# Q times K transposed for 96 heads: twelve-head blocks loaded one by one, or eight-head blocks loaded in pairs

## The chip, the cores and the metric

The kernel runs on one core of one Trainium2 chip. The metric is the device time of one execution in microseconds (us). Before the change the median of three runs is 1062.25 us (1062.21 to 1062.76). One more execution was profiled: it took 1061.68 us, and its span from the first to the last instruction is 1059.7 us, so 2.0 us lie around the span.

## The reference

```python
batch, n_heads, seq, head_dim = 8, 12, 1024, 64
q, k: float32 [8, 12, 1024, 64]

def reference(q, k):
    return np.einsum('bhid,bhjd->bhij', q, k).astype(np.float32)
```

For each of the 96 heads this is a 1024 x 1024 matrix of float32, 4 MB (4096 KB as the profile counts transfers). The inputs are 50.3 MB in all, the output is 402.7 MB.

## The kernel before

**Blocks of heads.** The 96 heads are worked in order. They are grouped in blocks (`sizes`, L33): 2, 2, 4, 8, 8 and then six blocks of 12. A block is what is loaded, cast and transposed together. The heads of one block are computed while the next block is being prepared.

**Loads.** The first three blocks are loaded into a tile `early` that borrows one of the three output buffers, the first two head by head (`load_head`), the third whole. From the fourth block on, `load` (L70 to L80) takes one of the two buffers of `in_pool` and moves Q, or K, of the whole block with one DMA. Each of the 128 partitions gets `N*S/128` consecutive rows of 64 floats, so one contiguous piece of 16 KB in a block of eight and of 24 KB in a block of twelve. Block 3 is loaded at the start, Q from SP's queue and K from ACT's. All later loads stand in a list `stream`; `next_load` takes the next one and issues it from ACT's queue. Two are taken (Q and K of one block) in one place of each block, given by `LOADS` (L353): head 1 of block 2, head 4 of blocks 3 and 4, head 6 of the later ones, always behind the second of that head's four copies on ACT. A load into a buffer waits until GpSimd has cast everything that was in it, and this wait stands in ACT's own instruction order: the copies behind it wait too.

**Casts.** GpSimd (POOL) turns a loaded block into float16, in chunks (`cast_quads`, L117 to L137). `cut` (L68) says into how many row groups a block is divided, so that a chunk fits a tile of `CHUNK` = 1536 float16 a partition; with two parts for each of Q and K that is eight chunks for a block of 8 or of 12. A chunk is four casts of 32 partitions. Chunks go to tiles of `half_pool`, of which there are five. `to_half` puts the casts into GpSimd's program as far as two blocks ahead.

**Transposes.** VectorE (DVE) transposes each chunk in 32 x 32 squares (`transpose_quads`, L143 to L149) into `qT` or `kT`, of which there are two sets (`tr_pool`), so that block i+1 is prepared while block i is read. VectorE's program holds nothing else but a few early copies. The first transpose of a block waits until TensorE has finished with the block two before it.

**Scores and stores.** For each head TensorE makes 16 matmuls of 128 x 512 (L175), two 1024-column rows of PSUM tile at a time; ACT copies 128 x 2048 from PSUM to `o_sb` four times (L185); SP then stores the head's 4 MB with one DMA of 128 pieces of 32 KB (L189). There are three `o_sb` buffers, so the copies of a head wait for the store of the head three before it. The seventh head from the end (`SPLIT`) is stored in parts from several queues (`split_scores`), one of them from a tile of `in_pool`.

Of the kernel before, what the change touches and what calls it, by code (L numbers as in the profile page):

```python
# [9 lines left out]
F32 = mybir.dt.float32  # L10
P = 128

@with_exitstack
def kernel(
# [6 lines left out]
    nc = tc.nc  # L21

    B, H, S, D = q.shape
    NT = S // P
    BH = B * H
# [3 lines left out]
    qf = q.rearrange("b h s d -> (b h s) d")  # L29
    kf = k.rearrange("b h s d -> (b h s) d")  # L30
    of = out.rearrange("b h i j -> (b h) i j")

    sizes = [2, 2, 4, 8, 8] + [12] * ((BH - 24) // 12)  # L33
    assert sum(sizes) == BH
    PE_BLOCKS = 2
    NMAX = max(sizes)
    CHUNK = 48 * 32
    SPLIT = BH - 7
    KEEP = 6

# [3 lines left out]
    spare = consts.tile([P, P], F16)  # L44

    in_pool = ctx.enter_context(tc.tile_pool(name="in_pool", bufs=2))
    half_pool = ctx.enter_context(tc.tile_pool(name="half_pool", bufs=5))
    tr_pool = ctx.enter_context(tc.tile_pool(name="tr_pool", bufs=2))
    out_pool = ctx.enter_context(tc.tile_pool(name="out_pool", bufs=3))

    pin = tc.keep_in_program_order

    def half_tile():
        half_sb = half_pool.tile([P, CHUNK], F16, tag="half")
        return half_sb

    class Block:
# [3 lines left out]
        def __init__(self, first, N, by_pe):  # L61
            self.first, self.N, self.by_pe = first, N, by_pe
            self.R = N * S // P
            self.elems = self.R * D
            self.raw = [None] * 2
            self.rows = [None] * 2
            self.halves = {}
            self.cut = max(1, self.R * 32 // CHUNK + (self.R * 32 % CHUNK > 0))  # L68

        def load(self, x, eng):  # L70
            if self.raw[x] is None:
                x_sb = in_pool.tile([P, self.elems], F32, tag="x")
                self.raw[x] = x_sb
            start = self.first * S
            src = (qf, kf)[x][start : start + self.N * S]
            pin(
                eng.dma_start(  # L77
                    out=self.raw[x], in_=src.rearrange("(p r) d -> p (r d)", p=P)
                )
            )  # L80

# [113 lines left out]
    def split_scores(b, n, ps_pool):  # L195
        half, g = divmod(n, b.N // 2)
        cs = slice(half * D, (half + 1) * D)
        qT = b.qT[cs, g * S : (g + 1) * S]
        kT = b.kT[cs, g * S : (g + 1) * S]
        dst = of[b.first + n]  # L200
        o_sb = out_pool.tile([P, NT, S], F32, tag="out")
        more_sb = in_pool.tile([P, NMAX * S // P * D], F32, tag="x")

        sorted_sb = half_tile()
        kept = KEEP * P
        groups = qT[:, kept:].rearrange("c (e s r t) -> c s t e r", s=2, r=4, t=4)
        columns = sorted_sb[cs, : 4 * P].rearrange("c (t m) -> c t m", t=4)
        for m in range(4):
            pin(
                nc.vector.tensor_copy(  # L210
                    out=columns[:, :, 32 * m : 32 * m + 32].rearrange(
                        "c t (e r) -> c t e r", r=4
                    ),
                    in_=groups[:, 1 - m // 2],
                )
            )
        for_five = slice(0, 64)
        pin(
            nc.gpsimd.dma_start(
                out=spare[:5, for_five].rearrange("p (a x) -> p a x", a=2)[:, :, :16],  # L220
                in_=ident[:5, for_five].rearrange("p (a x) -> p a x", a=2)[:, :, :16],
            )
        )

        def rows(to, count, weights, copy):
            ps = ps_pool.tile([P, 2 * S], F32, tag="po")
            for m, w in enumerate(weights):
                for j in range(2):
                    at = m * S + j * 512
                    pin(  # L230
                        nc.tensor.matmul(  # L231
                            ps[:count, at : at + 512], w, kT[:, j * 512 : j * 512 + 512]
                        )
                    )
            pin(copy(out=to, in_=ps[:count, : len(weights) * S]))  # L235

        flat = o_sb.rearrange("p t j -> p (t j)")
        first = qT[:, :kept].rearrange("c (p t) -> c t p", t=KEEP)
        for u in range(0, KEEP, 2):
            rows(  # L240
                flat[:, u * S : (u + 2) * S],
                P,
                [first[:, u], first[:, u + 1]],
                nc.scalar.copy,
            )
        pin(
            nc.sync.dma_start(
                out=dst[:kept].rearrange("(p t) j -> p (t j)", t=KEEP),
                in_=flat[:, : KEEP * S],
            )  # L250
        )
        for u in range(2):
            rows(
                more_sb[:, 3 * u * S : (3 * u + 2) * S],
                P,
                [columns[:, 2 * u], columns[:, 2 * u + 1]],
                nc.scalar.copy,
            )
        pairs = more_sb.rearrange("p (u t j) -> p u (t j)", u=2, j=S)[:, :, : 2 * S]
        blocks_of = dst[kept:].rearrange("(e s r t) j -> s e r (t j)", s=2, r=8, t=2)  # L260

        def part(eng, side, first, last):
            base = 64 * (1 - side)
            pin(
                eng.dma_start(  # L265
                    out=blocks_of[side, first:last],
                    in_=pairs[base + 4 * first : base + 4 * last],
                )
            )

        part(nc.gpsimd, 1, 5, 8)
        part(nc.gpsimd, 0, 0, 8)
        part(nc.sync, 1, 0, 4)
        left = kept + 9 * 16
        rows(flat[:16, KEEP * S : KEEP * S + S], 16, [qT[:, left : left + 16]], nc.scalar.copy)
        pin(nc.sync.dma_start(out=dst[left : left + 16], in_=flat[:16, KEEP * S : KEEP * S + S]))

    blocks, first = [], 0
# [7 lines left out]
    for b in blocks[:3]:  # L286
# [7 lines left out]
        else:  # L294
            for x in range(2):
                b.load(x, (nc.sync, nc.scalar)[x])
    stream = [(b, x) for b in blocks[3:] for x in range(2)]

    def next_load(eng):
        if stream:  # L300
            b, x = stream.pop(0)
            b.load(x, eng)

    for x in range(2):
        next_load((nc.sync, nc.scalar)[x])
    make_identity(nc, ident)

    casts = [
# [3 lines left out]
    def to_half(last):  # L312
        while casts:
            i, c = casts[0]
            if i > last or (blocks[i], c[0]) in stream:
                return
            blocks[i].cast_quads(*c)
            casts.pop(0)

    for b in blocks[:PE_BLOCKS]:  # L320
        for x in range(2):
            b.cast_rows(x)
    to_half(2)

    def block(i, heads, ps_pool, w):
        b = blocks[i]
        nxt = blocks[i + 1] if i + 1 < len(blocks) else None
        for n in heads:
            side = {}
            if nxt and nxt.by_pe:  # L330
                if n == 1:
                    side = {
                        u: [
                            lambda x=u // 2: nxt.transpose_rows(
                                x, ps_pool, nc.vector.tensor_copy
                            )
                        ]
                        for u in (1, 3)
                    }
            elif nxt:  # L340
                parts = nxt.chunks()
                some = [s for m, s in enumerate(parts) if m * b.N // len(parts) == n]
                side = {0: [lambda s=s: nxt.transpose_quads(*s) for s in some]}

            if n == LOADS.get(i, 6):
                side[1] = side.get(1, []) + [lambda: next_load(nc.scalar)] * 2
            if b.first + n == SPLIT:
                split_scores(b, n, ps_pool)
            else:
                b.scores(n, side, ps_pool, w)  # L350
            to_half(i + 2 + (n == b.N - 1))

    LOADS = {0: None, 1: None, 2: 1, 3: 4, 4: 4}  # L353

    blocks[0].alloc()
    blocks[1].alloc()
    with tc.tile_pool(name="first_pool", bufs=4, space=bass.MemoryType.PSUM) as pool:
        for x in range(2):
            blocks[0].transpose_rows(x, pool, (nc.vector.tensor_copy, nc.scalar.copy)[x])
        block(0, [0], pool, 1)  # L360
    po_pool = ctx.enter_context(
        tc.tile_pool(name="po_pool", bufs=2, space=bass.MemoryType.PSUM)
    )
    block(0, [1], po_pool, 2)
    for i in range(1, len(blocks)):
        if i + 1 < len(blocks):
            blocks[i + 1].alloc()
        block(i, range(blocks[i].N), po_pool, 2)
# [30 lines left out]
```

## Time and profile before

| what | value |
| --- | --- |
| median of three runs | 1062.25 us |
| profiled execution | 1061.68 us |
| its span | 1059.7 us |
| bytes read from and written to memory | 50.33 MB and 402.65 MB |
| mean rate over the span | 427 GB/s |
| store of a head: issues, size, median time from issue to landing | 95, 4096 KB, 21.8 us |
| load of a twelve-head Q: issues, size, median time to landing | 6, 3072 KB, 22.8 us |
| load of a twelve-head K: issues, size, median time to landing | 6, 3072 KB, 39.9 us |
| matmul L175, mean of 1520 | 617 ns |
| copy L185, 128 x 2048, mean of 376 | 1869 ns |
| cast L131, 32 x 1536, mean of 192 | 1460 ns |
| transpose L149, 128 x 1536, mean of 24 each for Q and K | 8065 and 8121 ns |

The engines' busy times overlap. A share of the span says how much an engine worked, not that it set the pace. MB are millions of bytes; the KB of a transfer are 1024 bytes. In the list of DMA queues q1 is the queue that SP issues to and q10 the one of ACT; "share of 16 engines" is the time of their packets over sixteen times the span.

### The profile page before, as it was taken

How to read it: one execution, taken by the hardware profiler on the slowest of the kernel's cores; microseconds unless marked ns; L12 is line 12 of the kernel's file. 1: busy time of each engine (PE TensorE's matmuls, PEld its weight loads, DVE VectorE, ACT ScalarE, POOL GpSimd, SP SyncE). 2: the span in 40 equal slices, each digit the busy share in tenths (PEclk: the TensorE clock that was granted, in tenths of full speed). 3: DMA queues.
4: the chain of work that ended last, by engine and by line, in shares of the span. 5: the costliest groups of instructions: out<-in, count | busy, mean ns of one | idle time of the engine just before them, and what ended most of it. 6: DMA issues, size and time to landing. Idle time of an engine off the chain costs nothing.

```text
span 1059.7 us, 4311 instructions
## 1 busy us (share of the span) xinstructions
PE 703.9 (66%) x1574; PEld 242.0 (23%) x1574; DVE 472.1 (45%) x79; ACT 700.2 (66%) x388; POOL 370.2 (35%) x289
## 2 busy tenths in 40 slices
PE   6866755764687367773777736778367787777870
PEld 2322211221222122221222212222122222222320
DVE  2999601992597006970069600796007960000000
ACT  4866755755677377783777746777467777777971
POOL 6959119606640372303733046330463300000000
DMA  9999999999999999999999999999999999999998
GB/s 382 429 431 436 435 425 438 429 431 426 435 434 426 432 430 432 434 426 421 437 434 434 411 433 436 431 432 427 430 432 434 431 432 429 433 433 434 426 429 357
DMA packets 17977, 453.26 MB, mean 428 GB/s; under 512 B 2204, under 2 KB 2204, under 8 KB 3244
## 3 DMA queue, kind: packets, MB, share of 16 engines
q1 hardware_dynamic: 14756, 406.13, 89.1%
q10 hardware_dynamic: 2880, 46.14, 10.4%
q0 software_dynamic: 320, 0.72, 0.2%
q8 instruction: 12, 0.20, 0.1%
q14 instruction: 9, 0.07, 0.0%
HBM read 50.33 MB, written 402.65 MB: 427 GB/s over the span
## 4 chain that ended last, share of the span: by engine, by line
DMA 69%; ACT 17%; PE 8%; DVE 2%; issue 1%; POOL 1%; ACTq 0%; SPq 0%
DMA out_dram<-o_sb 68%; ACT o_sb L185 17%; PE ps L175 8%; DVE qT L149 1%; DVE kT L149 1%; DMA early<-in_q_dram 0%; POOL half_sb L131 0%; PE ps L155 0%; POOL half_sb L101 0%; DVE kT L158 0%; DVE o_sb L183 0%; ACTq L185 0%; ACT kT L158 0%; SPq L88 0%; ACTq L77 0%
## 5 line engine op out<-in xcount | busy, mean ns | idle before, releaser
L185 ACT COPY o_sb<-ps 128x2048 f32<-128x2048 f32 (+1 forms) x380 | 687.8, 1860 | 326.7 <-DMA out_dram<-o_sb 285.0
L175 PE MATMUL ps<-kT,qT 64*128 64x512 f16 x1520 | 689.7, 617 | 321.3 <-ACT o_sb L185 316.6
L131 POOL CAST half_sb<-x_sb 32x1536 f16<-32x1536 f32 (+1 forms) x256 | 346.5, 1353 | 454.3 <-DMA x_sb<-in_q_dram 313.9
L175 PEld LDWEIGHTS <-qT 64*128 64x128 f16 x1520 | 235.8, 157 | 773.3 <-issue 768.9
L149 DVE STREAM_TRANSPOSE qT<-half_sb 128x1536 f16<-128x1536 f16 (+1 forms) x34 | 232.9, 7141 | 371.2 <-issue 371.2
L149 DVE STREAM_TRANSPOSE kT<-half_sb 128x1536 f16<-128x1536 f16 (+1 forms) x34 | 234.2, 7184 | 0.0
L265 POOL DMA_DIRECT2D out_dram<-more_sb x2 | 1.3, 648 | 150.2 <-ACT more_sb L235 150.2
L131 POOL CAST half_sb<-early 32x1024 f16<-32x1024 f32 x16 | 16.5, 1034 | 4.1 <-DMA early<-in_q_dram 3.4
L155 PE MATMUL ps<-ident,half_sb 128*128 128x128 f16 x32 | 4.1, 309 | 6.9 <-POOL half_sb L101 6.3
L231 PE MATMUL ps<-kT,qT 64*128 64x512 f16 (+1 forms) x14 | 6.5, 615 | 2.5 <-ACT o_sb L235 2.3
L235 ACT COPY o_sb<-ps 128x2048 f32<-128x2048 f32 (+1 forms) x4 | 6.5, 1650 | 2.5 <-DMA out_dram<-o_sb 2.3
L158 DVE COPY qT<-ps 128x1024 f16<-128x1024 f16 x2 | 2.4, 1224 | 12.4 <-PE ps L155 12.4
L183 DVE COPY o_sb<-ps 128x1024 f32<-128x1024 f32 x4 | 4.9, 1224 | 4.3 <-PE ps L175 4.3
L101 POOL CAST half_sb<-early 128x512 f16<-128x512 f32 x8 | 4.6, 614 | 4.1 <-DMA early<-in_q_dram 4.1
L155 PEld LDWEIGHTS <-half_sb 128*128 128x128 f16 x32 | 3.2, 141 | 8.7 <-POOL half_sb L101 6.6
L158 ACT ACT_TABLE_LOAD x1 | 1.3, 1283 | 5.9 <-DMA early<-in_q_dram 5.9
L231 PE MATMUL ps<-kT,half_sb 64*128 64x512 f16 x8 | 3.7, 615 | 0.2 <-ACT o_sb L235 0.2
L235 ACT COPY more_sb<-ps 128x2048 f32<-128x2048 f32 x2 | 3.7, 1866 | 0.1
L231 PEld LDWEIGHTS <-qT 64*128 64x128 f16 (+1 forms) x14 | 1.8, 134 | 7.1 <-issue 7.1
L158 DVE COPY kT<-ps 128x1024 f16<-128x1024 f16 x1 | 1.2, 1225 | 4.3 <-PE ps L155 4.3
L158 ACT COPY kT<-ps 128x1024 f16<-128x1024 f16 x1 | 1.0, 1012 | 1.2 <-PE ps L155 1.2
L231 PEld LDWEIGHTS <-half_sb 64*128 64x128 f16 x8 | 1.1, 133 | 2.7 <-issue 2.7
(8 smaller groups left out, 2.4 us busy)
## 6 DMA issues: line engine op xcount, KB each, us to landing
out_dram<-o_sb SPq DMA_DIRECT2D x95, 4096.0 KB, 21.8
x_sb<-in_q_dram ACTq DMA_DIRECT2D x6, 3072.0 KB, 22.8
x_sb<-in_k_dram ACTq DMA_DIRECT2D x6, 3072.0 KB, 39.9
x_sb<-in_k_dram ACTq DMA_DIRECT2D x2, 2048.0 KB, 22.0
out_dram<-o_sb SPq DMA_DIRECT2D x1, 3072.0 KB, 21.3
x_sb<-in_q_dram SPq DMA_DIRECT2D x1, 2048.0 KB, 17.8
x_sb<-in_q_dram ACTq DMA_DIRECT2D x1, 2048.0 KB, 19.1
early<-in_k_dram ACTq DMA_DIRECT2D x4, 256.0 KB, 4.5
```

Of the source, the lines that this page charges most:

```text
L101: nc.gpsimd.tensor_copy(out=self.rows[x][:, :, half], in_=self.raw[x][:, half * n : (half + 1) * n].rearrange("p (r d) -> p r d", d=D),)
L131: nc.gpsimd.tensor_copy(out=half_sb[q0 : q0 + 32].rearrange("p (r d) -> p r d", d=32), in_=raw[32 * b : 32 * b + 32, c * m : (c + 1) * m, h],)
L149: pin(nc.vector.transpose(out=dst, in_=src))
L155: pin(nc.tensor.transpose(t_ps[:, t], self.rows[x][:, t], ident))
L158: pin(copy(out=dst, in_=src))
L175: nc.tensor.matmul(ps[:, at : at + 512], qT[cs, g, w * u + tt], kT[cs, g, js],)
L183: pin(nc.vector.tensor_copy(out=dst, in_=ps))
L185: pin(nc.scalar.copy(out=dst, in_=ps))
L231: nc.tensor.matmul(ps[:count, at : at + 512], w, kT[:, j * 512 : j * 512 + 512])
L235: pin(copy(out=to, in_=ps[:count, : len(weights) * S]))
L265: eng.dma_start(out=blocks_of[side, first:last], in_=pairs[base + 4 * first : base + 4 * last],)
```

## The change

Blocks are now 2, 2, 4 and then eleven blocks of eight. Block 3 is still loaded alone at the start, Q from SP and K from ACT, but both go into one tile `shared` of `in_pool`. The other ten blocks of eight are loaded in five pairs: one DMA moves Q of two blocks, one DMA moves K of two blocks, 4 MB each, and a partition gets two pieces of 16 KB that lie 2 MB apart in memory. A pair's two loads are issued from ACT at head 3 of blocks 2, 4, 6, 8 and 10, behind the second copy of that head. Each buffer of `in_pool` grows from 24 KB to 32 KB a partition; `qT` and `kT` shrink from 12 KB to 8 KB each; there are seven chunk tiles of 2 KB instead of five of 3 KB. All chunks of eight-head blocks have 1024 float16 a partition, eight to a block, so one is transposed with each head. The tile that `split_scores` takes from `in_pool` has the new size, of which the same 24 KB are used.

```diff
-    sizes = [2, 2, 4, 8, 8] + [12] * ((BH - 24) // 12)
+    sizes = [2, 2, 4] + [8] * ((BH - 8) // 8)
...
-    CHUNK = 48 * 32
+    RAW = 2 * NMAX * S // P * D
+    CHUNK = 32 * 32
...
-    half_pool = ctx.enter_context(tc.tile_pool(name="half_pool", bufs=5))
+    half_pool = ctx.enter_context(tc.tile_pool(name="half_pool", bufs=7))
...
-            self.cut = max(1, self.R * 32 // CHUNK + (self.R * 32 % CHUNK > 0))
+            self.cut = max(1, self.R * 32 // CHUNK)
...
+        def load_two(self, other, x, eng):
+            x_sb = in_pool.tile([P, RAW], F32, tag="x")
+            m = self.elems
+            self.raw[x], other.raw[x] = x_sb[:, :m], x_sb[:, m:]
+            start = self.first * S
+            src = (qf, kf)[x][start : start + 2 * self.N * S]
+            pin(
+                eng.dma_start(
+                    out=x_sb.rearrange("p (u e) -> p u e", u=2),
+                    in_=src.rearrange("(u p r) d -> p u (r d)", u=2, p=P),
                 )
             )
...
-        more_sb = in_pool.tile([P, NMAX * S // P * D], F32, tag="x")
+        whole = in_pool.tile([P, RAW], F32, tag="x")
+        more_sb = whole[:, : 6 * S]
...
-    stream = [(b, x) for b in blocks[3:] for x in range(2)]
+    shared = in_pool.tile([P, RAW], F32, tag="x")
+    for x in range(2):
+        n = blocks[3].elems
+        blocks[3].raw[x] = shared[:, x * n : (x + 1) * n]
+        blocks[3].load(x, (nc.sync, nc.scalar)[x])
+    pairs = [blocks[i : i + 2] for i in range(4, len(blocks), 2)]
+    assert all(len(pair) == 2 for pair in pairs)
+    stream = [(pair, x) for pair in pairs for x in range(2)]
 
     def next_load(eng):
         if stream:
-            b, x = stream.pop(0)
-            b.load(x, eng)
-
-    for x in range(2):
-        next_load((nc.sync, nc.scalar)[x])
+            (b, other), x = stream.pop(0)
+            b.load_two(other, x, eng)
+
...
-            if n == LOADS.get(i, 6):
+            if n == (3 if i % 2 == 0 and i > 0 else None):
                 side[1] = side.get(1, []) + [lambda: next_load(nc.scalar)] * 2
...
-    LOADS = {0: None, 1: None, 2: 1, 3: 4, 4: 4}
```

More of the change, by code (lines that the diff above doesn't have):

```diff
@@ L67, in __init__ @@
             self.halves = {}
-            self.cut = max(1, self.R * 32 // CHUNK + (self.R * 32 % CHUNK > 0))
+            self.cut = max(1, self.R * 32 // CHUNK)
         def load(self, x, eng):
-            if self.raw[x] is None:
-                x_sb = in_pool.tile([P, self.elems], F32, tag="x")
-                self.raw[x] = x_sb
             start = self.first * S
@@ L78, in load @@
                     out=self.raw[x], in_=src.rearrange("(p r) d -> p (r d)", p=P)
+                )
+            )
+        def load_two(self, other, x, eng):
[8 more added lines that the diff above has]
+                    in_=src.rearrange("(u p r) d -> p u (r d)", u=2, p=P),
                 )
@@ L314, in to_half @@
             i, c = casts[0]
-            if i > last or (blocks[i], c[0]) in stream:
+            if i > last or blocks[i].raw[c[0]] is None:
                 return
```

## The prediction

> **What bounds the kernel now.** I read the page from the top: busy times, slices, queues, the chain.
>
> ```profile
> span 1059.7 us, 4311 instructions
> PE 703.9 (66%) x1574; PEld 242.0 (23%) x1574; DVE 472.1 (45%) x79; ACT 700.2 (66%) x388; POOL 370.2 (35%) x289
> ...
> DMA  9999999999999999999999999999999999999998
> GB/s 382 429 431 436 435 425 438 429 431 426 435 434 426 432 430 432 434 426 421 437 434 434 411 433 436 431 432 427 430 432 434 431 432 429 433 433 434 426 429 357
> ...
> q1 hardware_dynamic: 14756, 406.13, 89.1%
> q10 hardware_dynamic: 2880, 46.14, 10.4%
> ...
> DMA 69%; ACT 17%; PE 8%; DVE 2%; issue 1%; POOL 1%; ACTq 0%; SPq 0%
> ...
> L185 ACT COPY o_sb<-ps 128x2048 f32<-128x2048 f32 (+1 forms) x380 | 687.8, 1860 | 326.7 <-DMA out_dram<-o_sb 285.0
> ```
>
> No compute engine is busy for more than 66%, while the DMA engines are busy in every slice and the packets of q1 and q10 fill 99.5% of their time. ACT's idle time is mostly a wait for stores (285.0 of 326.7 us). The chain shows ACT at 17% because it passes through the copies between two stores; meanwhile two other stores are in the queue. So the end is set by a sum: all packets, one after another on sixteen engines, plus a start and a ragged end. An edit counts only if it changes the time of the packets or lets the engines run dry.
>
> Next I cut the span into stretches with and without loads (engine columns: busy time and count; the last three are clock, DMA share and GB/s).
>
> ```profile
> 59.00:89.00 30.00, 19.28 (x43) 6.27 (x41) 29.16 (x7) 18.22 (x10) 19.22 (x20) 1.00 1.01 435
> 134.00:169.00 35.00, 17.52 (x40) 6.09 (x39) 0.00 (x0) 17.56 (x11) 14.26 (x10) 1.00 1.01 432
> 390.00:465.00 75.00, 55.85 (x124) 19.02 (x123) 57.90 (x8) 56.19 (x31) 18.36 (x13) 1.00 1.00 433
> 604.00:639.00 35.00, 18.07 (x41) 6.24 (x40) 0.00 (x0) 18.09 (x11) 14.73 (x11) 1.00 1.00 421
> 1040.00:1060.00 20.00, 0.00 (x0) 0.00 (x0) 0.00 (x0) 0.00 (x0) 0.00 (x0) 1.00 0.76 326
> ```
>
> Seven stretches of stores alone (100 to 1040 us without the loads) give 432.3 GB/s by their lengths; the third line is one. The first line is the pair of 16 KB loads of block 4: 435, no loss. The six bursts of 24 KB loads run at 432, 428, 429, 422, 421 and 424; at 432.3 they would have taken 0.0, 0.3, 0.3, 0.9, 0.9 and 0.7 us less, together 3.1 us, 0.52 each. In the trace's packet records this lies mostly in the first 5 us of a burst, where 24 KB packets take 1.1 to 2.1 us instead of the usual 0.912.
>
> **The change part by part.**
>
> *Packets.* The same bytes move. In the packet records 32 KB take 1.213 us, 24 KB 0.912, 16 KB 0.611 (medians). 16 KB more cost 0.602, so a packet costs 0.009 us beside its bytes. Blocks 4 and later were 256 packets of 16 KB and 1536 of 24 KB; now they are ten loads of 256 packets of 16 KB. 768 more at 0.009 over 16 engines: **+0.43 us**.
>
> *Bursts.* Instead of six 24 KB bursts and one of 16 KB there are five of 8.39 MB. Their loss is not in the trace. Lower end: none, as in the one 16 KB burst, −3.1. Upper end: the worst burst (0.91 us for 6.29 MB) by bytes, 1.21 each, 6.1, so +3.0. I take one mean loss per burst, since the loss sits at the start: 5 x 0.52 = 2.6, **−0.5 us**.
>
> *Load issue.* ACT's wait in block 2 goes:
>
> ```profile
> 56.43 0.33 ACTq L77 DMA_DIRECT2D x_sb<-in_q_dram  x1
> 66.02 0.33 ACTq L77 DMA_DIRECT2D x_sb<-in_k_dram  x1
> 66.39 3.64 ACT L185 COPY o_sb<-ps 128x2048 f32<-128x2048 f32 x2 [8.12 <-POOL half_sb L131]
> ```
>
> ACT stood 8.1 us because the K load needed block 3's casts to be done; behind it stood the copies, their stores and TensorE. It gives **0**: the DMA engines were busy throughout. Now the pair is issued two heads later. Copies go at about 7.64 us a head (46.97 to 54.65), so head 3's second copy runs at about 72, when the casts (done at 66) have freed the buffer.
>
> *Is the first pair in time?* From the slices, 29.7 MB have moved by 72 us; less 8.39 of early loads that is 5.1 stores of 4.19 MB. Block 4's first copies need fourteen stores done: 8.9 x 9.7 us and 19.4 us for the pair's bytes, so at about 178. Sharing the engines packet by packet, 16 KB against 32 KB, a load gets a third (34.6% between 66 and 82 us), 0.144 MB/us. Q and K take 29 us each; with 5 us of lead (the 2 MB Q load landed after 19.1, its bytes needing 14) K is there at 135. The rows for the rest:
>
> ```profile
> L131 POOL CAST half_sb<-x_sb 32x1024 f16<-32x1024 f32 x64 | 66.1, 1034 | 13.4 <-DMA x_sb<-in_q_dram 9.7 <-DVE qT L149 0.9
> L149 DVE STREAM_TRANSPOSE qT<-half_sb 128x1024 f16<-128x1024 f16 x10 | 46.7, 4924 | 0.8 <-issue 0.8
> ```
>
> Four chunks of four casts, 16.5 us, and a last transpose of 4.9: 156. That is 22 us early. If it were late, ACT's wait would first eat the queue: when ACT starts a head, two stores are queued (19.4 us); filling takes 7.6 and the lead 5, so 7 us are covered. Later pairs have twelve heads, 136 us, against 63 + 21. Their buffers are free, because the last cast of a pair needs only the first transpose of its second block, and that runs three heads before the issue. Behind ACT's two issues stand copies; a longer issue (1.2 us for K now) is within the cover. SP's order is unchanged.
>
> *Casts and transposes.* POOL: 352 casts of 1.034 us, 364 for 346.4 before; DVE: 92 transposes of 4.93, 454 for 467. Transposing a block takes 39.5 us within at least 77.5 (eight heads): covered by stores, **0**. Without that cover, the 17.6 us of POOL would be the price.
>
> *End.* The same last heads, with the split. By the packet records the first engine finishes 3.4 us before the last; whether the last one has a packet more or less is one 32 KB packet, **0 ± 1.2 us**.
>
> *Sum.* +0.4 − 0.5 = −0.1 on the profiled execution: 1061.68 becomes 1061.6. The median stands 0.57 above that execution, so I predict **1062.1 us**. The ends are −3.1 + 0.4 − 1.2 = −3.9 and +3.0 + 0.4 + 1.2 = +4.6, so this case alone runs from 1058.4 to 1066.9. About 0.2% (2.1 us) is what a measurement here can tell from no change: below 1060.1 is faster, above 1064.4 slower.
>
> **The rivals.**
>
> *Calm bursts (faster).* If 16 KB loads lose nothing, as between 59 and 89 us, the 3.1 us go and only the packets are paid: −2.7, 1059.6. For it: that stretch's 435 GB/s, and two bursts fewer. Against it: that burst was early, and the early 24 KB bursts lost little too; the loss grew to 0.9 later.
>
> *Two places that collide (slower).* The sixteen engines walk their partitions alike, and each alternates between places 2 MB apart. If that keeps up the disorder of a burst's first microseconds, the pair runs throughout at the worst burst's rate: 8.39 MB at 0.144 is 58 us, 2.6% of it 1.5 us, five times 7.6, less 3.1 plus 0.4: +4.9, 1067.2. It decides from 0.96 us lost per pair ((3.1 − 0.4 + 2.1) / 5), which is a rate below 425 in the burst. For it: the loss of a start is there. Against it: it fades within 5 us, and no load before has two places. The Trainium skill, "DMA: Bandwidth & Descriptors", section "Latency and other measured facts", says that copies whose partitions lie 2 MiB apart ran at 164 GB/s instead of 207, which it puts down, unverified, to memory channels that lock-stepped streams share; taken for every 16 KB load packet that would be an estimate of 25.6 us more, 1087.7. Here partitions lie 16 KB apart and only a partition's two pieces 2 MB, so the rule speaks half against this change, and no stretch of the trace tests that half.
>
> *A wait that starves the queue (slower).* An ACT wait, at an issue or for the first pair's transposes, that goes beyond the 7 us. A K landing 22 + 20 us late would cost 13 us: 1075. For it: the 8.1 us above show that such waits happen. Against it: all margins are 20 us or more.
>
> **How the numbers follow.** Forecast 0.55, calm bursts 0.19, collision 0.18, starving 0.08. Everything in the forecast's case within 2.1 us counts as same; what its own ends reach beyond is what the first two rivals price. So faster 0.19, same 0.55, slower 0.26. The range takes in the forecast's ends and this collision, and leaves out starving and a strong collision: 1058.4 to 1067.2.
>
> **What would show it.** DMA 9 in every slice and the wait of ACT still for stores: the bound is unchanged. Load packets on q10 up by 768 less 64 for four DMAs fewer, to 3584: the packet step. GB/s in the five bursts: near 430 is the forecast, 432 calm, below 425 collision. ACT's idle time by POOL gone, and block 4's first copies waiting for a store, not for DVE. Wrong would be a slice with DMA under 9 after the first, or a wait of ACT or TensorE on L160's transposes.

## The result, and the profile after

The changed kernel takes **1069.43 us** (median of six runs, 1067.97 to 1071.83) against 1062.51 for the kernel before in the same series: a ratio of 1.0063, 95% interval 1.0053 to 1.0073. The forecast was no change, 1062.1, with a range up to 1067.2; the time lies 2.2 us above that range. The profiled execution of the changed kernel took 1067.97 us, its span is 1066.2 us, 6.5 more than before. It is the shortest of the six, so the further 1.5 us of the median stand in no trace.

The page of the changed kernel, with the lines that answer to those shown of before (L196 is the copy that was L185):

```profile
span 1066.2 us, 4425 instructions
PE 703.8 (66%) x1574; PEld 241.1 (23%) x1574; DVE 435.1 (41%) x103; ACT 700.1 (66%) x388; POOL 387.6 (36%) x385
...
DMA  9999999999999999999999999999999999999997
GB/s 379 435 432 430 426 433 435 433 419 422 430 431 434 433 421 420 427 434 433 433 433 412 424 430 431 432 434 433 411 427 434 432 433 433 431 433 433 414 432 324
...
q1 hardware_dynamic: 14756, 406.13, 89.1%
q10 hardware_dynamic: 3584, 46.14, 10.2%
...
DMA 71%; ACT 18%; PE 8%; issue 1%; DVE 0%; POOL 0%; ACTq 0%; SPq 0%
...
L196 ACT COPY o_sb<-ps 128x2048 f32<-128x2048 f32 (+1 forms) x380 | 687.7, 1859 | 334.0 <-DMA out_dram<-o_sb 304.6
```

The bound is the same: DMA engines busy in every slice, ACT waiting for stores. The queue q10 has 3584 packets as counted beforehand. Nothing ran dry. No wait of ACT or TensorE was added, and ACT's wait for POOL is gone; VectorE now waits 36.5 us for casts, but TensorE waits no longer for its transposes than before (0.2 us). So the 6.5 us are in the packets and in the ragged end, and the GB/s row shows where: dips to 411 to 427 in the slices of the later four bursts (the 9th and 10th, the 15th to 17th, the 22nd and 23rd, the 29th and 30th).

The same kernel cut into its five bursts of loads, and two stretches of stores alone (columns as before: busy times, clock, DMA share, GB/s):

```profile
76.00:132.00 56.00, 28.40 (x63) 9.59 (x62) 26.86 (x6) 26.52 (x15) 16.53 (x16) 1.00 1.00 426
214.00:272.50 58.50, 28.21 (x63) 9.60 (x62) 1.27 (x1) 26.84 (x16) 16.54 (x16) 1.00 1.00 421
392.00:449.00 57.00, 27.77 (x62) 9.39 (x61) 0.83 (x1) 26.18 (x16) 16.54 (x16) 1.00 1.00 420
568.00:627.00 59.00, 28.53 (x64) 9.64 (x63) 1.60 (x1) 27.94 (x16) 16.53 (x16) 1.00 1.00 419
746.00:804.00 58.00, 28.05 (x63) 9.52 (x62) 0.58 (x1) 28.08 (x17) 16.53 (x16) 1.00 1.00 418
140.00:210.00 70.00, 52.43 (x117) 18.05 (x116) 49.79 (x11) 51.49 (x29) 44.81 (x44) 1.00 1.00 433
280.00:390.00 110.00, 81.25 (x180) 27.69 (x179) 69.03 (x16) 81.19 (x45) 45.28 (x44) 1.00 1.00 433
```

All engines are busy (DMA share 1.00) in the bursts too, and yet the bursts move 1.6 to 3.5% less by these rows. The packet records tell which packets are longer. I call a packet slow when it takes over 0.05 us more than the median of its size. In the bursts of the kernel before, 3.0% of the 32 KB stores and 5.2% of the loads were slow; in those of the changed kernel 13.6% of the stores and 0.7% of the loads, and not at the start of a burst but all through its 58 us. A store there takes 1.251 us on average, 1.217 between the bursts.

Against the rate of the stores alone in the same trace (432.5 GB/s) the bursts lose 6.8 us, before 3.4. I work this from the packet records, with the part of a packet that lies inside a burst, from its first load packet to its last; rows cut at whole microseconds, as above, are uncertain by a per cent or so at their edges. The records also show two kinds of loss. One sits at the start: between the issue of the loads and the first load packet, and just behind it, some packets take about twice as long. What packets take beyond the medians of their sizes, summed over all bursts and shared out over the sixteen engines, comes to 0.9 us before and 1.6 after in the 6 us ahead of the first load packets. The other kind goes on for as long as the loads run: beyond the first 6 us of the bursts it is 1.0 us before and 5.2 after. This second kind is what grew most.

The end also changed. The last steps of the changed kernel that move anything, and those of before, with the DMA share in the column ahead of GB/s:

```profile
1056.00:1058.00 2.00, 0.00 (x0) 0.00 (x0) 0.00 (x0) 0.00 (x0) 0.00 (x0) 1.00 0.88 377
1058.00:1060.00 2.00, 0.00 (x0) 0.00 (x0) 0.00 (x0) 0.00 (x0) 0.00 (x0) 1.00 0.53 229
1060.00:1062.00 2.00, 0.00 (x0) 0.00 (x0) 0.00 (x0) 0.00 (x0) 0.00 (x0) 1.00 0.27 115
1062.00:1064.00 2.00, 0.00 (x0) 0.00 (x0) 0.00 (x0) 0.00 (x0) 0.00 (x0) 1.00 0.30 131
```

```profile
1053.00:1054.00 1.00, 0.00 (x0) 0.00 (x0) 0.00 (x0) 0.00 (x0) 0.00 (x0) 1.00 0.99 426
1054.00:1055.00 1.00, 0.00 (x0) 0.00 (x0) 0.00 (x0) 0.00 (x0) 0.00 (x0) 1.00 0.38 164
1055.00:1056.00 1.00, 0.00 (x0) 0.00 (x0) 0.00 (x0) 0.00 (x0) 0.00 (x0) 1.00 0.31 131
1056.00:1057.00 1.00, 0.00 (x0) 0.00 (x0) 0.00 (x0) 0.00 (x0) 0.00 (x0) 1.00 0.23 98
```

Before, most engines finish together and a few run on for 3 us. After, they thin out over some 7 us. By the packet records the first and the last engine end 3.4 us apart before and 7.7 after; from the mean end to the last it is 2.2 and 4.7. The sum of all packets over sixteen engines grew from 1057.3 to 1062.3 us. So of the 6.5 us of the span, 5.0 are longer or more packets, 3.4 of them in the bursts, and the other 1.5 go with the more uneven end.

### The profile page after: what moved, and what is told of

Same layout as the page of the kernel before. It is cut to its first block, busy times and chain, and to the rows that moved or that the text cites. A ratio compares the mean times of both kernels' runs of the same rounds, so it can differ in the third digit from the quotient of the medians.

```text
span 1066.2 us, 4425 instructions
## 1 busy us (share of the span) xinstructions
PE 703.8 (66%) x1574; PEld 241.1 (23%) x1574; DVE 435.1 (41%) x103; ACT 700.1 (66%) x388; POOL 387.6 (36%) x385
## 3 DMA queue, kind: packets, MB, share of 16 engines
q10 hardware_dynamic: 3584, 46.14, 10.2%
## 4 chain that ended last, share of the span: by engine, by line
DMA 71%; ACT 18%; PE 8%; issue 1%; DVE 0%; POOL 0%; ACTq 0%; SPq 0%
DMA out_dram<-o_sb 70%; ACT o_sb L196 17%; PE ps L186 8%; DMA early<-in_q_dram 0%; PE ps L243 0%; ACT o_sb L247 0%; PE ps L166 0%; ACT whole L247 0%; POOL half_sb L112 0%; DVE kT L169 0%; DVE o_sb L194 0%; ACTq L196 0%; ACT kT L169 0%; SPq L277 0%; SPq L99 0%
## 5 line engine op out<-in xcount | busy, mean ns | idle before, releaser
L196 ACT COPY o_sb<-ps 128x2048 f32<-128x2048 f32 (+1 forms) x380 | 687.7, 1859 | 334.0 <-DMA out_dram<-o_sb 304.6
L142 POOL CAST half_sb<-x_sb 32x1024 f16<-32x1024 f32 x320 | 330.7, 1033 | 500.0 <-DMA x_sb<-in_q_dram 276.7
L160 DVE STREAM_TRANSPOSE qT<-half_sb 128x1024 f16<-128x1024 f16 x46 | 214.4, 4936 | 458.0 <-issue 431.8
L160 DVE STREAM_TRANSPOSE kT<-half_sb 128x1024 f16<-128x1024 f16 x46 | 216.4, 4989 | 10.3 <-POOL half_sb L142 10.3
L142 POOL CAST half_sb<-shared 32x1024 f16<-32x1024 f32 x32 | 33.1, 1034 | 1.5
L169 DVE COPY qT<-ps 128x1024 f16<-128x1024 f16 x2 | 2.4, 1224 | 12.3 <-PE ps L166 12.3
L247 ACT COPY whole<-ps 128x2048 f32<-128x2048 f32 x2 | 3.7, 1865 | 0.1
## 6 DMA issues: line engine op xcount, KB each, us to landing
x_sb<-in_q_dram ACTq DMA_DIRECT2D x5, 4096.0 KB, 34.7
x_sb<-in_k_dram ACTq DMA_DIRECT2D x5, 4096.0 KB, 63.1
```

The lines of the kernel that those rows point to most:

```text
L142: nc.gpsimd.tensor_copy(out=half_sb[q0 : q0 + 32].rearrange("p (r d) -> p r d", d=32), in_=raw[32 * b : 32 * b + 32, c * m : (c + 1) * m, h],)
L160: pin(nc.vector.transpose(out=dst, in_=src))
L169: pin(copy(out=dst, in_=src))
L196: pin(nc.scalar.copy(out=dst, in_=ps))
```

## The experiments

Theories A (two places in one DMA), B (16 KB pieces: B1 by their spacing in memory, B2 by the size of the packet) and C (long bursts) came first; D and E, D1 and D2 grew out of the answers. The table has what each run gave; burst loss and slow share are worked from the packet records of its profile as above, over the loads from block 4 on. The ratio is to the kernel before, timed on the same chip. Each profile is one execution: the six kernels whose 16 KB loads come from ACT's queue beside 32 KB stores (changed, e1, e3 to e6) lose 4.5 to 7.1 us with packets of the same sizes, so a difference within that spread is not read as an effect.

| kernel | load packets | median us | ratio, 95% interval | burst loss us | slow stores in bursts |
| --- | --- | --- | --- | --- | --- |
| before | 1536 x 24 KB, 256 x 16 KB | 1062.3 to 1062.9 | | 3.4 | 3.0% |
| changed | 2560 x 16 KB | 1069.43 | 1.0063, 1.0053 to 1.0073 | 6.8 | 13.6% |
| e1_two_dmas | 2560 x 16 KB | 1067.50 | 1.0049, 1.0032 to 1.0065 | 7.1 | 13.1% |
| e2_one_place | 1280 x 32 KB | 1062.79 | 1.0002, 0.9992 to 1.0011 | 2.9 | 0.5% |
| e3_far | 2560 x 16 KB | 1069.54 | 1.0068, 1.0053 to 1.0083 | 5.4 | 10.9% |
| e4_singles | 2560 x 16 KB | 1066.48 | 1.0040, 1.0025 to 1.0054 | 4.9 | 8.8% |
| e5_pitch18 | 2560 x 16 KB | 1068.67 | 1.0060, 1.0043 to 1.0077 | 6.0 | 12.0% |
| e6_one_place_16k | 2560 x 16 KB | 1066.23 | 1.0033, 1.0020 to 1.0046 | 4.5 | 10.8% |
| e7_overlap | 1280 x 32 KB | 1062.51 | 0.9998, 0.9988 to 1.0007 | 3.0 | 1.3% |
| e8_pieces_8k | 5120 x 8 KB | 1066.56 | 1.0038, 1.0025 to 1.0051 | 4.9 | 7.0% |
| e9_loads_by_sp | 2560 x 16 KB, no turns | 1064.44 | 1.0017, 1.0008 to 1.0026 | 3.2 | 0.0% |
| e10_before_by_sp | as before, no turns | 1064.96 | 1.0021, 1.0012 to 1.0030 | 3.5 | 0.2% |
| e11_before_12k | 3072 x 12 KB, 256 x 16 KB | 1069.75 | 1.0070, 1.0056 to 1.0083 | 7.7 | 12.3% |
| e12_stores_16k | 2560 x 16 KB, stores 16 KB | 1067.06 | 1.0042, 1.0024 to 1.0059 | 1.4 | 0.7% |

What goes on beyond the first 6 us of the bursts, worked as in the section before, parts the kernels more clearly: 1.0 to 1.6 us with 24 or 32 KB loads in ACT's queue (before, e2, e7), 2.8 to 6.1 with loads of 16, 12 or 8 KB there (changed, e1, e3 to e6, e8, e11), and 0.3 in e12. In e9 and e10 it is 2.8 and 3.2, but in slow loads, not in stores.

### Two places, the size of a piece, or the length of a burst

e1_two_dmas, in place of `load_two`'s DMA:

```diff
-            start = self.first * S
-            src = (qf, kf)[x][start : start + 2 * self.N * S]
-            pin(
-                eng.dma_start(
-                    out=x_sb.rearrange("p (u e) -> p u e", u=2),
-                    in_=src.rearrange("(u p r) d -> p u (r d)", u=2, p=P),
-                )
-            )
+            self.load(x, eng)
+            other.load(x, eng)
```

> The changed kernel, but each 4 MB load of a pair is issued as two 2 MB DMAs, first the one block, then the other, into the same two halves of the buffer. The packets (16 KB, 2560), the issue points and the 8.39 MB bursts stay; only no engine alternates any more between two places 2 MB apart. Theory A (the alternation between the two places slows the stores beside it): the five bursts go back from 418 to 426 GB/s to about 430, and the time to 1062 to 1064 us. Theory B (16 KB pieces, which put the engines' reads 64 KB apart, whatever the order): bursts stay near 420, time near 1069. Theory C (long bursts of 8.39 MB let the engines drift apart): stays near 1069 too.

It stayed slow: 1067.5 us, with bursts losing 7.1. One place at a time does not help, and the size of the pieces and the length of the bursts, which theories B and C blame, are as they were. That its median is below the changed kernel's says little, since the intervals overlap.

e2_one_place:

```diff
-                    out=x_sb.rearrange("p (u e) -> p u e", u=2),
-                    in_=src.rearrange("(u p r) d -> p u (r d)", u=2, p=P),
+                    out=x_sb, in_=src.rearrange("(p r) d -> p (r d)", p=P)
```

> The changed kernel with the same ten 4 MB loads, but each partition gets one piece of 32 KB from one place (the rows of the pair's heads come to other partitions than the casts suppose, so other rows are multiplied). Theory A (two places) and theory B (16 KB pieces): bursts back to about 430 GB/s, time 1061 to 1064 us. Theory C (long bursts): bursts of 8.39 MB stay, so near 420 GB/s and 1069 us, or a little less since a 32 KB load shares the engines half and half and the burst is 39 us long.

The whole difference went: 1062.79, the interval of the ratio holds 1. Everything else of the change is in this kernel, so blocks of eight, seven chunk tiles, smaller casts and transposes and the issue points cost nothing that can be measured. Its five bursts in the windows view:

```profile
75.50:112.50 37.00, 16.53 (x37) 5.64 (x37) 20.29 (x5) 16.36 (x10) 15.17 (x15) 1.00 0.99 428
212.00:249.00 37.00, 15.63 (x36) 5.25 (x35) 1.22 (x1) 15.65 (x9) 14.69 (x15) 1.00 1.01 433
389.00:427.00 38.00, 16.19 (x37) 5.45 (x36) 0.86 (x1) 16.04 (x10) 14.67 (x15) 1.00 1.00 421
566.00:605.00 39.00, 18.13 (x41) 6.13 (x40) 0.92 (x1) 18.15 (x11) 16.09 (x16) 1.00 1.00 426
742.00:782.00 40.00, 19.11 (x44) 6.53 (x43) 1.24 (x1) 19.14 (x11) 15.30 (x15) 1.00 1.00 420
```

They are some 39 us long, because a 32 KB load takes half of the engines' time instead of a third. The rate was not back to 430 in all of them: the third and the fifth run at 421 and 420, as low as in the changed kernel, in part by what is lost at their starts and by window edges. What tells the two kernels apart is the loss beyond the first 6 us, 1.3 us here against 5.2. A single row's GB/s does not.

e3_far, with the second place 40 KB further:

```diff
-            src = (qf, kf)[x][start : start + 2 * self.N * S]
+            far = self.N * S + 160
+            start = min(start, BH * S - 2 * far)
+            src = (qf, kf)[x][start : start + 2 * far]
+            src = src.rearrange("(u y) d -> u y d", u=2)[:, : self.N * S]
...
-                    in_=src.rearrange("(u p r) d -> p u (r d)", u=2, p=P),
+                    in_=src.rearrange("u (p r) d -> p u (r d)", p=P),
```

> The changed kernel with the second place 2 MB + 40 KB away in place of 2 MB (the second block of a pair gets other rows). Still one DMA, two places, 16 KB. Theory A in the form that the distance, a power of two, makes the two places collide: 1062 to 1064 us, bursts near 430. Theory A in the form that two places in one DMA cost whatever their distance, theory B and theory C: near 1069, bursts near 420.

1069.54: the distance of 2 MB is not it. With e1 and e3, theory A is out.

e4_singles, on the kernel before:

```diff
-    sizes = [2, 2, 4, 8, 8] + [12] * ((BH - 24) // 12)
+    sizes = [2, 2, 4] + [8] * ((BH - 8) // 8)
...
-            if n == LOADS.get(i, 6):
+            if n == LOADS.get(i, 4):
```

> The kernel before with blocks 2, 2, 4 and eleven of eight, each block loaded alone by two DMAs of 2 MB in 16 KB pieces, at head 1 of block 2 and head 4 of the later blocks. Ten bursts of 4.19 MB, 29 us each, in place of five of 8.39 MB. Theory A: no two places, so bursts at 430 and more, 1061 to 1064 us. Theory B: bursts near 420, as long in all as those of the changed kernel, so 1068 to 1070. Theory C: the bursts are short, 1062 to 1064.

1066.48 and 4.9 us lost, between what B and C expected. The ten short bursts last 299 us in all, the five long ones 288. Halving the bursts does not cure the loss, so C is not what makes it. Whether the length of a burst has a part in its size is not shown: 4.9 lies inside the spread of the kernels with five long bursts (4.5 in e6, 7.1 in e1).

### Spacing in memory, or the size of the packet

e5_pitch18 reads 64 rows of every 72; e6_one_place_16k cuts e2's 32 KB in two by a gap of 32 bytes in the buffer; e7_overlap reads 32 KB from starts 16 KB apart; e8_pieces_8k takes four places (the lines that make the difference):

```diff
+            src = src.rearrange("(u p r) d -> p u r d", u=2, p=P)[:, :, : self.R]    # e5, r = 72
...
+                    out=x_sb.rearrange("p (u e) -> p u e", u=2)[:, :, :m],           # e6
+                    in_=src.rearrange("(p u r) d -> p u (r d)", u=2, p=P),           # e6
...
+            src = bass.AP(src.tensor, src.offset, [[self.elems, P], [1, 2 * self.elems]])  # e7
...
+                    in_=src.rearrange("(u p r) d -> p u (r d)", u=4, p=P),           # e8
```

> The changed kernel, its pair loads still of 256 pieces of 16 KB from two places, but the pieces of neighbouring partitions start 18 KB apart in memory and not 16 (the blocks get other rows, the second place lies 2.25 MB away). Theory B1 (the spacing in memory, 16 KB, a power of two, makes the engines' reads and the stores' writes meet): bursts back to 428 to 432 GB/s, 1062 to 1064 us. Theory B2 (the size of the packet, wherever it comes from): bursts near 420, 1067 to 1070 us.

> As e2_one_place, 32 KB in a row for each partition, but cut into two packets of 16 KB (the two halves of the buffer stand 32 bytes apart; other rows are multiplied). Theory B1 (spacing): the partitions are 32 KB apart as in e2, so 1062 to 1064 us. Theory B2 (packet size): bursts near 420, stores beside the loads as slow as in the changed kernel, 1067 to 1070 us.

> The changed kernel with ten 4 MB loads of 128 pieces of 32 KB whose starts lie 16 KB apart, so that neighbouring partitions read overlapping rows (other rows are multiplied). Theory B1 (spacing): near 1067 to 1070 us. Theory B2 (packet size): as e2, 1062 to 1064 us.

> The changed kernel with pieces of 8 KB from four places 1 MB apart, 5120 load packets in place of 2560 (other rows are multiplied). Theory B2 (packet size): the loss in the bursts grows again by about as much as from 24 to 16 KB, so 6.9 us become 10 to 14, and the time 1073 to 1078 us. A theory in which the cost of 16 KB is a special case of that size or of its spacing: 1062 to 1070 us.

e7 has the spacing of the changed kernel and packets of 32 KB: 1062.51. e5 has packets of 16 KB and another spacing: 1068.67. e6 has e2's one place and spacing and packets of 16 KB: 1066.23, between the two ranges that were given for it, but with 10.8% of its stores slow, as B2 has it. The size of the packet decides, and B1 is out. But e8 failed B2's dose: twice as many packets of 8 KB gave 1066.56 and 4.9 us lost, no more than 16 KB, where 10 to 14 were expected. It is not a fixed price per load packet.

### Turns

In the bursts of the changed kernel load packets and store packets come in turn. Between 580 and 620 us of its trace the two queues passed the same number of packets (the third figure is the share of the engines' time):

```profile
q1 hardware_dynamic: 376, 10.88, 65.6%
q10 hardware_dynamic: 376, 5.90, 34.5%
```

Theory D puts the loss down to these turns, theory E does not. With both in one queue there should be none. e9_loads_by_sp (on the changed kernel) and e10_before_by_sp put the loads into SP's; e11_before_12k cuts the twelve-head loads of the kernel before:

```diff
-                side[1] = side.get(1, []) + [lambda: next_load(nc.scalar)] * 2
+                side[1] = side.get(1, []) + [lambda: next_load(nc.sync)] * 2         # e9, e10
...
+                    out=self.raw[x].rearrange("p (u e) -> p u e", u=2),              # e11, blocks of 12 alone
+                    in_=src.rearrange("(u p r) d -> p u (r d)", u=2, p=P),           # e11
```

> The changed kernel with the pairs' loads issued from SP's queue instead of ACT's, at the same head. On one queue an engine works off the loads in one go, between two stores, and no longer one load packet and one store packet in turn. Theory D (it is the turn-taking of 16 KB load packets with stores that slows the stores): the slow stores beside the loads go, at most the start of each burst stays, 1062 to 1065 us. Theory E (16 KB loads cost the same however they are queued): 1067 to 1070 us. Loads in one go could also starve nothing but delay two stores by 20 us, which the engines do not notice.

> The kernel before with its 24 KB loads issued from SP's queue. Theory D: the 3.1 us that its bursts lose have little to do with turns (they lie in the first microseconds), so between 1060 and 1063 us. Theory E: no change, 1062 to 1063.

> The kernel before, the loads of its twelve-head blocks cut into pieces of 12 KB (two places 1.5 MB apart, so other rows are multiplied): 3072 load packets in place of 1536, everything else as it was. Theory B2 (load packets of 16 KB and less slow the stores in any kernel): bursts lose 5 to 7 us in place of 3.1, and the time is 1065 to 1069 us. If the loss came from what else the change did (blocks of eight, chunks, buffers): 1062 to 1064 us, the packets alone costing 1536 x 0.009 / 16 = 0.9.

In e9 none of the stores that begin in the load stretches is slow any more (336; in the changed kernel 2432 begin there), with the same 2560 packets of 16 KB, and the sum of packets falls from 1062.3 to 1057.4 us. Theory D holds for that part. The 3.2 us that its bursts still lose lie in the loads, of which 4.7% are slow, and not at the start of the stretches. The time falls by 5 us to 1064.44, still 2.2 above the kernel before with the same sum of packets; its end is more uneven, the last engine 6.3 us after the mean against 2.2. e10 missed what both theories gave it: 1064.96, slower than the kernel before with the same sum of packets (1057.3), and again with an uneven end (5.6). Why the loads' queue makes the end uneven was not tried.

e11 puts the whole loss into the kernel before by the size of the pieces alone: 1069.75 and 7.7 us lost, both a little above what was expected. Three of its six twelve-head bursts:

```profile
344.00:396.00 52.00, 28.03 (x62) 9.61 (x61) 0.00 (x0) 26.29 (x16) 22.98 (x16) 1.00 1.00 423
476.00:529.00 53.00, 28.80 (x64) 9.94 (x63) 0.00 (x0) 27.19 (x16) 22.76 (x16) 1.00 1.01 421
...
741.00:795.00 54.00, 28.73 (x64) 9.92 (x63) 0.00 (x0) 28.69 (x17) 23.38 (x16) 1.00 1.01 419
```

With 24 KB these bursts were 35 us long; now they are 53 and lose all along, as the changed kernel's do.

e12_stores_16k, on the changed kernel:

```diff
+            for part in range(2):
+                cols = slice(part * 4 * S, (part + 1) * 4 * S)
                 pin(
                     nc.sync.dma_start(
-                        out=of[self.first + n].rearrange("(p t) j -> p (t j)", p=P),
+                        out=of[self.first + n].rearrange("(p t) j -> p (t j)", p=P)[:, cols],
-                        in_=o_sb.rearrange("p t j -> p (t j)"),
+                        in_=o_sb.rearrange("p t j -> p (t j)")[:, cols],
```

> The changed kernel with each head's store (but the split one) issued as two DMAs of 128 pieces of 16 KB, so that loads and stores take turns in packets of one size. 12160 more packets at 0.009 us over 16 engines make some 6.8 us more everywhere, so the time says little; the bursts are to be read against the stretches of stores alone in the same run (near 429 GB/s by the extra packets). Theory D1 (a load packet of 16 KB or less slows whatever store takes turns with it): bursts 2 to 3% below the stores alone, as in the changed kernel, time 1074 to 1080 us. Theory D2 (what counts is that the load packet is short against the 32 KB store): bursts within 1% of the stores alone, 1066 to 1072 us.

1067.06, in D2's range although 12160 more store packets are in it, and below the changed kernel. Its five bursts, and a stretch of stores alone:

```profile
75.00:115.00 40.00, 17.81 (x40) 6.13 (x40) 22.83 (x6) 17.93 (x11) 16.55 (x16) 1.00 1.01 432
213.00:253.00 40.00, 17.98 (x40) 6.00 (x40) 0.73 (x1) 17.82 (x10) 16.55 (x16) 1.00 1.01 423
391.00:430.00 39.00, 18.53 (x42) 6.13 (x41) 0.07 (x1) 18.52 (x11) 16.55 (x16) 1.00 1.00 421
568.00:607.00 39.00, 17.29 (x40) 5.80 (x38) 0.00 (x0) 17.31 (x11) 16.46 (x16) 1.00 1.01 421
745.00:785.00 40.00, 19.62 (x45) 6.70 (x44) 0.28 (x1) 18.70 (x11) 16.55 (x16) 1.00 1.01 421
258.00:388.00 130.00, 94.41 (x208) 32.29 (x208) 71.11 (x16) 94.84 (x53) 46.46 (x45) 1.00 1.01 431
```

By these rows four bursts run some 2% below the stores alone, which was D1's sign. The rows begin 1 to 2 us ahead of the first load packet, and the packet records show that the loss sits there: worked as above, 2.9 us over the five bursts come in the 6 us ahead of the first load packets (1.6 in the changed kernel), and only 0.3 us beyond the first 6 us of the bursts (5.2). Inside the bursts 1.4 us are lost against the stores alone (429.8 GB/s), and 0.7% of the stores are slow. So with 16 KB against 16 KB the loss all through the burst is gone, as D2 has it, and the one at the start is not; with 16, 12 or 8 KB against 32 KB the first is there.

## Why the prediction was wrong

**What held.** The bound; 3584 packets on q10; ACT's wait gone; the pair in time. (A head's copies take 7.68 us by the two rows named for 7.64; nothing hangs on it.) The issue was put at 72 us and came at 73.5; K was to land after 63 us:

```profile
x_sb<-in_q_dram ACTq DMA_DIRECT2D x5, 4096.0 KB, 34.7
x_sb<-in_k_dram ACTq DMA_DIRECT2D x5, 4096.0 KB, 63.1
```

The median from issue to landing is 63.1 us for K and 34.7 for Q (34 by the same working). Casts and transposes stayed covered, and e2 and e7 show that price of nothing directly.

**What failed: the step "Bursts".** "I take one mean loss per burst, since the loss sits at the start: 5 x 0.52 = 2.6". Measured: 6.8, above even the upper end of 6.1; against the 3.4 of the kernel before, worked the same way, the term is +3.4 us where −0.5 stood. The loss of 24 KB bursts does sit mostly at their start, in slow load packets. The changed kernel has another one, which the trace of before could hardly show: slow stores, all through the burst, when short load packets take turns with 32 KB stores. The only 16 KB burst of before was calm, and so was the changed kernel's first (0.5 of the 6.8 us); the four later ones lost 1.4 to 1.8 each. I let that early stretch stand for the lower end, "none, as in the one 16 KB burst", though the profile's own rows showed early bursts calm at 24 KB too.

**The end** was put at 0 ± 1.2 us and missed too: the last engine is 4.7 us behind the mean against 2.2, and 1.5 us of the span are left when the 5.0 of the packets are taken off. e9 and e10 show that an end can grow while the stores beside the loads are not slow, so this is a second term, and what sets it is open.

**The rival that came nearest** was the collision: its sign (bursts below 425 GB/s, four of five), its shape (disorder all through the burst) and its size (+4.9, 1067.2, 2.2 us short) were close. Its cause was not: e1 and e3 took away the alternation and the 2 MB, and the stores stayed slow. The rule cited there from the Trainium skill, "DMA: Bandwidth & Descriptors", section "Latency and other measured facts", does not describe this case: the loads themselves stayed at 0.613 us a packet on average (0.611 the median before), and changed pitches (e3, e5) stayed slow.

**Open.** What inside an engine or at the memory makes a 32 KB store slow beside short loads is not shown; nor why 8 KB, with twice the packets, hurts no more than 16; nor why the later bursts lose more than the first; nor what makes packets slow between the issue of loads and their first packet; nor what makes the end uneven. No version beat the kernel before.

## What to carry to other kernels

In this kernel DMA is the bound and loads stand in another queue than the stores; the engines took turns packet by packet, and the sizes of the two packets were a choice like a tile size: 24 or 32 KB loads beside 32 KB stores cost 3 us in 1062, 8 to 16 KB ones 4.5 to 8. The layout that made the DMA larger while its pieces grew smaller was a loss; look at the bytes in a row for each partition, not at the size of the DMA. And when every DMA engine is busy, compare the rate of a stretch with that of a quiet one: a busy share of 1.00 hid packets that take longer.

## What the runs showed of the hardware that was not expected

- Slow packets change sides with the size of the load: with 32 KB loads (e2) 7.7% of the loads and 0.5% of the stores in the bursts are slow, with 16 KB loads (changed) 0.7% and 13.6%.
- It takes two queues: with both on SP's queue (e9) none of the 336 stores that begin in the load stretches is slow.
- It takes a load packet that is short against the store's: in the bursts 16 KB loads beside 16 KB stores (e12) lose 1.4 us, beside 32 KB stores 6.8 (changed).
- Loads cost something before their first packet: in the some 4 us between the issue and that packet, many store packets took up to about twice their median, which came to 2.9 us over the five bursts of e12.
- With equal sums of packets the end can differ by some 3 us, through engines that finish unevenly: 1057.3 us of packets end in a span of 1059.7 (before) and of 1062.8 (e10).
